# Attention layer of a hybrid decode step: turned weights fetched earlier, decode attention later, another order of output tiles

## The chip, the cores and the metric

The kernel runs on one core of one Trainium2 chip. The metric is the device time of one execution, in microseconds (us). The kernel before has a median of 1266.56 us over 3 runs (1266.55 to 1269.77).

## The reference, cut to what matters

A prompt of 1024 tokens and 8 single new tokens ("decode") go through two layers: a retention layer and a sliding-window attention layer (SWA). The change touches the SWA layer alone:

```
h = rmsnorm(x, g_norm); proj = h @ w_in                       # 1024 -> 1024 q, 128 k, 128 v, 1024 gate
q, k = rmsnorm per head (16 q heads of 64, 2 kv heads)
scores = q k^T / 8 - slope*dist, band of 128 keys back, one sink column per head
p = softmax(scores | sink);  o = p v                          # prompt, and likewise decode over cache_k, cache_v
y = x + (o * silu(gate)) @ w_out
```

All products must hold fp32 accuracy, so a projection is three matmuls: high part of the weights by high part of x, high by low, low by high (`proj`, L1698 to L1700).

## The kernel before, in words

The order of the work on each engine is written out by hand (a manual schedule): every engine's queue holds its instructions in the order in which the Python code emits them, and an engine waits at the head of its queue.

**Weights.** `wslot` (L1632) brings a block of 256 weight columns in four pieces of 256 KB. `load(i)` is a DMA on SP (SyncE's queue) into one of three buffers `wr` (L1642); `conv(i)` is a copy on ACT that makes the high part `wh` (L1648) and a subtraction on POOL that makes the low part `wl` (L1649). The fourth load needs a buffer that the first conversion has freed. A slot's steps stand in its list `todo`; `job()` takes from it up to the next `None` or to the next conversion, so a `None` is a pause of one job place.

**Projection tiles.** `group_proj` and later `so_all` are generators that emit projection tiles: a tile is 8 times the three matmuls into one of two PSUM banks `pj`. `fill(src, W)` pulls about W = 1.03 us of matmuls from them. A finished q tile is emptied by ACT (a square, L1915, and a scaled copy, L1916), a gate tile by DVE (L1930), then ACT (L1935) and DVE (L1941). `soon` and `now()` hold small pieces of work back to the next place.

**Attention.** 32 units of work ("duos": 4 head pairs pp by 8 chunks c of 128 tokens) go through one period each. In period m:

- PE: `att_o` of duo m-2 if its pp is odd (40 matmuls, L2108, which read the turned weights `R`), then `att_s` of duo m (scores, L2053), then four or five fills.
- DVE and ACT: `att_out` and `att_split` of duo m-2 (L2118, L2133, L2137 or L2141), `att_e` of duo m (bias and maximum, L2069 and L2074), `att_p` (four exponentials on ACT, L2080), `att_r` (reciprocal L2084, product on POOL L2085).
- `att_x` of the duo of period m-1: for even pp a DVE transpose into `pb` and a DMA of it to `pbs` in HBM (L2090, L2091); for odd pp a DMA of the even half back from `pbs` into `R` (L2094) and a DVE transpose of the odd half into `R` (L2095). `R` has two buffers.
- `ms_mm` and `ms_ev` (sums of squares of a q tile, L1991 to L2017) when a q pair is done; for the last third of the tokens (ti = 2) four small DMAs take the decode part `ms` to `ms16` (L2010).
- three job places a period, behind the first, second and fourth fill.

Decode attention is cut into steps (`dec_norm`, `dec_scores`, `dec_soft` 0 to 6, `dec_vload`, `dec_pt`, `dec_o`, `dec_out`; L2152 to L2229); the table `STEPS` says in which period and place each is emitted. `dec_out` sets `oready[2]`, without which no output tile of ti = 2 begins.

**Output tiles.** `so_all` emits 24 tiles (ft, ti): 8 blocks of 128 output columns by three groups of tokens. Each needs its residual loaded (`xr`, L2317), is summed on DVE (L2330), turned (L2260) and sent out in four DMAs (L2263). A tile with ti = 2 is also turned on PE (L104) for its decode rows.

When the last duo of group 0 is through, eight DMAs of 128 KB load the values of the second kv head (`kv_v4`, L1824).

Of the kernel before, what the change touches and what calls it, by code (L numbers as in the profile page):

```python
# [16 lines left out]
ND = 8  # L17
# [50 lines left out]
def _trunk(ctx, tc, nc, a):  # L68
# [1561 lines left out]
    def wslot(src, turn=True):  # L1630

        slot, box = [], {}  # L1632

        def first():
            box["hi"] = wp.tile([128, 8, 256], F32R, tag="wh", bufs=3, name="wh")
            box["lo"] = wp.tile([128, 8, 256], F32R, tag="wl", bufs=3, name="wl")
            slot[0:0] = (box["hi"], box["lo"])

        def load(i):
            raw = box[i] = wp.tile([128, 2, 256], F32, tag="wr", bufs=3, name="wr")  # L1640
            rows = src[256 * i:256 * i + 256]
            nc.sync.dma_start(out=raw, in_=rows.rearrange("(p u) f -> p u f", u=2) if turn else  # L1642
                              rows.rearrange("(k p) f -> p k f", p=128))

        def conv(i):
            js = slice(2 * i, 2 * i + 2)
            raw = box[i]
            nc.scalar.activation(box["hi"][:, js, :], raw, AF.Copy)  # L1648
            nc.gpsimd.tensor_tensor(box["lo"][:, js, :], raw, box["hi"].bitcast(F32)[:, js, :], ALU.subtract)  # L1649

        box["todo"] = [(first,), (load, 0), (load, 1), (load, 2), None, None, None, (conv, 0), (load, 3)] + [
            (conv, i) for i in range(1, 4)]
        jobs.append(box)
        slot.append(box)
        return slot
# [252 lines left out]
    def group_proj(gr):  # L1908

        def q_ev(pp, pl, ti, ps):  # L1910
            t0, t1 = TG[ti]
            n, npr = t1 - t0, min(t1, NP) - t0
            qs = Q[pp, ti, pl] = atp.tile([128, 384], F32, name="qs", bufs=6)
            sq = SQ[pp, ti, pl] = io("sq", 4)
            nc.scalar.activation(sq[:, :n], ps[:, :n], AF.Square)  # L1915
            nc.scalar.activation(qs[:, :npr], ps[:, :npr], AF.Copy, scale=gq)  # L1916
            if ti == 2:
                gs = slice(64 * gr, 64 * gr + 64)
                h = 4 * pp + 2 * pl
                nc.scalar.activation(Qd[gs, h, :], ps[lo_, 256:264], AF.Copy, scale=gq[lo_])  # L1920
                nc.scalar.activation(Qd[gs, h + 1, :], ps[hi_, 256:264], AF.Copy, scale=gq[hi_])
            if pl == 1:
                msq.append((pp, ti))

        def g_ev(pp, pl, ti, ps):
            t0, t1 = TG[ti]
            n, npr, nch = t1 - t0, min(t1, NP) - t0, chunks(ti)
            p = 2 * pp + pl
            gx = io("sq", 4)
            nc.vector.tensor_tensor(gx[:, :n], ps[:, :n], rbc[:, t0:t1], ALU.mult)  # L1930
            if p % 4 == 0:
                G[gr, ti] = atq[0].tile([128, 1536], F32, name="gt", bufs=2)
            gt = G[gr, ti].rearrange("p (n l x) -> p n l x", l=4, x=32)[:, 0:4 * nch, p % 4, :]
            gv = gx[:, :npr].rearrange("p (n x) -> p n x", x=32)
            nc.scalar.activation(gt, gv, AF.Tanh, scale=0.5)  # L1935
            gd, gxd = gdec2[:, p, :], gx[:, npr:n]
            if ti == 2:
                nc.scalar.activation(gd, gxd, AF.Tanh, scale=0.5)

            def rest():  # L1940
                nc.vector.scalar_tensor_tensor(gt, gt, 1.0, gv, ALU.add, ALU.mult)  # L1941
                if ti == 2:
                    nc.vector.scalar_tensor_tensor(gd, gd, 1.0, gxd, ALU.add, ALU.mult)
                    nc.vector.tensor_scalar(gd, gd, 0.5, None, ALU.mult)
            soon.append((rest,))

        a_, b_ = 2 * gr, 2 * gr + 1
        order = [("q", a_, 0), ("q", a_, 1), ("q", a_, 2), ("g", a_, 0), ("q", b_, 0), ("g", b_, 0), ("q", b_, 1),
                 ("q", b_, 2), ("g", a_, 1), ("g", b_, 1), ("g", a_, 2), ("g", b_, 2)]
        if gr == 0:  # L1950
            order.insert(10, ("q", 2, 0))
        else:
            order.pop(0)
        for kind, pp, ti in order:
            isq = kind == "q"
            t0, t1 = TG[ti]
            n = t1 - t0
            while 3 * (pp if isq else gr) + ti - (done["s"] if isq else done["o"]) >= (3 if isq else 2):
                yield 1e9
            for f in range(2):  # L1960
                ps = pjp.tile([128, 512], F32, tag="pj", name="pj")
                for k in range(8):
                    proj(ps[:, :n], slots[kind, pp], f, t0, t1, first=(k == 0), last=(k == 7), ks=[k])
                    if k < 7:
                        yield 3 * n / 2400.0
                (q_ev if isq else g_ev)(pp, f, ti, ps)
                if f == 1 and (kind, pp, ti) in nxt:
                    nxt[kind, pp, ti]()
                yield 3 * n / 2400.0
            if (kind, pp) == ("g", 3):  # L1970
                pend_r.append(ti)
# [29 lines left out]
    def ms_ev(xy, pp, ti, sq):  # L2001
        nch = chunks(ti)
        m = 32 * nch
        for j in range(2):
            nc.vector.transpose(sq[:, 192 * j:192 * j + 2 * m], xy[:, j, 320:320 + 2 * m])
        if ti == 2:
            ms = atp.tile([1, 2, 2, ND], F32, name="ms", bufs=1)
            nc.vector.tensor_copy(ms, xy[0:1, :, 448:464].rearrange("p j (l r) -> p l j r", l=2))
            for h in range(4):
                nc.sync.dma_start(out=ms16[4 * pp + h:4 * pp + h + 1, :], in_=ms[:, h // 2, h % 2, :])  # L2010
        rqf = atq[0].tile([128, 12], F32, name="rq", bufs=3)[:, 0:4 * nch]
        rq = rqf.rearrange("p (j l c) -> p j l c", j=2, l=2)
        mt = sq[:, 0:384].rearrange("p (j n) -> p j n", j=2)[:, :, 0:2 * m].rearrange(
            "p j (n i) -> p j n i", i=32)
        c0 = TG[ti][0] // 128
        for j in range(2):
            nc.vector.scalar_tensor_tensor(  # L2017
                rq[:, j], mt[:, j, :, 0].rearrange("p (l c) -> p l c", l=2), 1.0 / HD,
                e9[:, c0:c0 + nch].unsqueeze(1).broadcast_to([128, 2, nch]), ALU.mult, ALU.add)
        rsq(rqf, rqf, 4 * nch)  # L2020
        RQ[pp, ti] = rq
# [65 lines left out]
    def att_x(u):  # L2087
        if u.pp % 2 == 0:
            pb = atp.tile([128, 4, 160], F32, name="pb", bufs=1)
            nc.vector.transpose(pb, u.st[:, :, 0:160])  # L2090
            nc.sync.dma_start(out=pbs[u.c], in_=pb.rearrange("p h n -> p (h n)"))  # L2091
        else:
            u.pb = atp.tile([128, 2, 4, 160], F32, tag="R", name="R", bufs=2)
            nc.sync.dma_start(out=u.pb[:, 0].rearrange("p h n -> p (h n)"), in_=pbs[u.c])  # L2094
            nc.vector.transpose(u.pb[:, 1], u.st[:, :, 0:160])  # L2095

    def att_o(u):
        po = u.po = pvp.tile([128, 4, 512], F32, tag="o", name="o")
# [184 lines left out]
            nc.scalar.dma_start(out=y_s[:, 0, ft * 128:ft * 128 + 128], in_=yo[:8, 256:384])  # L2283

    def so_all():
        order = [(ft, ti) for ti in range(3) for ft in range(6)] + [(ft, ti) for ft in (6, 7) for ti in range(3)]
        early = []

        def start(ft, ti):
# [138 lines left out]
    dec_new()  # L2428
    while not msq:
        next(ps)  # L2430
    tq.close()
    xq_ = ExitStack()
    xyp = xq_.enter_context(tc.tile_pool(name="xyp", bufs=1, space=PSUM))
# [11 lines left out]
    def both():  # L2445
# [5 lines left out]
    W = 1.03  # L2451
    NU = len(duos)
    pend_m, x = [], None
    STEPS = {(30, 0): (dec_norm, 0), (30, 2): (dec_norm, 1), (30, 3): (dec_scores,), (30, 4): (dec_soft, 0),
             (31, 0): (dec_soft, 1), (31, 1): (dec_soft, 2), (31, 2): (dec_soft, 3), (31, 3): (dec_soft, 4),
             (31, 4): (dec_soft, 5), (32, 0): (dec_soft, 6), (32, 1): (dec_vload,), (33, 0): (dec_pt,), (33, 3): (dec_o,),
             (33, 4): (dec_out,)}

    def decode(m, s):
        if (m, s) in STEPS:  # L2460
            fn, *args = STEPS[m, s]
            fn(*args)

    for m in range(NU + 2):
        W = 0.95 if 16 <= m < 27 else 1.03
        u = duos[m] if m < NU else None
        w = duos[m - 2] if m >= 2 and duos[m - 2].pp % 2 else None
        if u:
            while (u.pp, u.ti) not in RQ:
                if msq:  # L2470
                    xy = xy_tile()
                    ms_ev(xy, *msq[0], ms_mm(xy, *msq.pop(0)))
                else:
                    next(ps)
        if w:
            assert (w.g, w.ti) in G
            att_o(w)
        if u:
            xy = xy_tile()
            att_s(u, xy)  # L2480
            if msq:
                pend_m.append((ms_ev, (xy, *msq[0], ms_mm(xy, *msq.pop(0)))))
        if w:
            att_out(w)
            att_split(w, 0)
# [29 lines left out]
        decode(m, 2)  # L2515
        fill(src, W)
        now()
        if u:
            att_r(u)
        decode(m, 3)  # L2520
# [53 lines left out]
```

## Time and profile before

| | us |
|---|---|
| median of 3 runs | 1266.56 |
| profiled execution | 1267.68 |
| span of its trace | 1265.9 |
| PE busy | 1224.4 (97%) |
| DVE, ACT, POOL busy | 743.2, 588.4, 688.7 |
| the stretch 880 to 1266 us (SWA layer): PE busy | 355.15 of 386.00 |
| the same: DVE, ACT, POOL busy | 194.86, 138.67, 140.36 |

The profile is of one execution. PE is busy almost throughout; the layer that the change touches takes the last 386 us. What is read below are the places in it where PE stands still or runs at half its clock. "a <- b" in a row of waits means that an instruction of a waited for b.

### The profile page before, as it was taken

What the parts mean: (1) busy time and instruction counts of PE and PEld (TensorE: products, weight loads), DVE (VectorE), ACT (ScalarE), POOL (GpSimd) and SP (SyncE); (2) the same over time, 40 slices, a digit from 0 to 9 for tenths busy, and PEclk for the clock granted to TensorE, in tenths of its full rate; (3) what the DMA queues carried; (4) which work ended last, traced back from release to release, by engine and by line L of the source; (5) the groups of instructions that cost most, each with busy time, mean ns of one, the idle gap of its engine ahead of it and who ended that gap; (6) DMA issues with size and microseconds to landing.
All of it is one profiled execution on the core that took longest, in us unless ns stands there. A gap on an engine that the chain in (4) does not pass through costs nothing.

```text
span 1265.9 us, 29416 instructions
## 1 busy us (share of the span) xinstructions
PE 1224.4 (97%) x11304; PEld 1159.7 (92%) x11304; DVE 743.2 (59%) x1462; ACT 588.4 (46%) x1482; POOL 688.7 (54%) x740
## 2 busy tenths in 40 slices
PE   7999999999999999999999999999999989987998
PEld 6999999999999999978889999999898978976998
DVE  7944655665565765377774566684265665667321
ACT  6533445454455554478772225454544454533000
POOL 6654444535458899889772357735555255334010
PEclk9999999999999999999999999999998999998999
DMA  6313867687666784465887955764322435153444
GB/s 219 110 59 121 256 183 227 195 252 211 196 205 192 225 231 133 124 207 175 259 249 193 294 166 183 232 191 118 108 76 95 119 114 145 68 193 106 112 106 88
DMA packets 260106, 213.10 MB, mean 168 GB/s; under 512 B 72905, under 2 KB 230981, under 8 KB 259950
## 3 DMA queue, kind: packets, MB, share of 16 engines
q1 hardware_dynamic: 210800, 178.16, 47.9%
q10 hardware_dynamic: 49166, 33.06, 8.8%
q8 instruction: 89, 1.46, 0.5%
q14 instruction: 51, 0.42, 0.1%
HBM read 139.03 MB, written 73.17 MB: 168 GB/s over the span
## 4 chain that ended last, share of the span: by engine, by line
PE 83%; DVE 5%; DMA 3%; POOL 3%; issue 3%; ACT 2%; SPq 1%; ACTq 0%; POOLq 0%; DVEq 0%
PE S L1317 9%; PE b L334 7%; PE b L336 7%; PE b L335 7%; PE pj L1698 6%; PE pj L1700 6%; PE pj L1699 5%; PE b L327 4%; PE b L328 4%; PE b L329 4%; PE tr L104 2%; PE o L2108 2%; PE b L543 2%; PE xy L2053 1%; DMA wr<-in_w_in_swa_dram 1%
## 5 line engine op out<-in xcount | busy, mean ns | idle before, releaser
L334 PE MATMUL b<-xh,woh 128*128 128x258 f32 x784 | 223.2, 285 | 0.0
L336 PE MATMUL b<-xh,wol 128*128 128x258 f32 x784 | 221.8, 283 | 0.2 <-POOL wol L225 0.2
L335 PE MATMUL b<-xl,woh 128*128 128x258 f32 x784 | 221.6, 283 | 0.0
L1698 PE MATMUL pj<-SA,wh 128*128 128x384 f32 (+1 forms) x576 | 193.4, 336 | 2.3 <-ACT qs L1916 2.1
L1700 PE MATMUL pj<-SA,wl 128*128 128x384 f32 (+1 forms) x576 | 187.6, 326 | 3.3 <-POOL wl L1649 3.3
L1699 PE MATMUL pj<-SA,wh 128*128 128x384 f32 (+1 forms) x576 | 187.0, 325 | 1.3 <-issue 1.3
L334 PEld LDWEIGHTS b<-xh,woh 128*128 128x128 f32 x784 | 148.0, 189 | 4.1 <-issue 4.1
L335 PEld LDWEIGHTS b<-xl,woh 128*128 128x128 f32 x784 | 148.7, 190 | 0.0
L336 PEld LDWEIGHTS b<-xh,wol 128*128 128x128 f32 x784 | 148.0, 189 | 0.4 <-POOL wol L225 0.4
L225 POOL TENSOR_TENSOR wol<-raw,woh 128x512 fp32r<-128x512 f32 x51 | 67.1, 1325 | 117.9 <-ACT woh L220 106.7
L327 PE MATMUL b<-woh,xh 128*128 128x256 f32 x448 | 126.6, 283 | 0.0
L328 PE MATMUL b<-wol,xh 128*128 128x256 f32 x448 | 126.0, 281 | 0.0
L329 PE MATMUL b<-woh,xl 128*128 128x256 f32 x448 | 125.6, 280 | 0.0
L1698 PEld LDWEIGHTS pj<-SA,wh 128*128 128x128 f32 x576 | 111.1, 193 | 11.1 <-issue 6.3
L1700 PEld LDWEIGHTS pj<-SA,wl 128*128 128x128 f32 x576 | 111.2, 193 | 5.1 <-POOL wl L1649 3.7
L1699 PEld LDWEIGHTS pj<-SA,wh 128*128 128x128 f32 x576 | 111.4, 193 | 0.0
L1649 POOL TENSOR_TENSOR wl<-wr,wh 128x512 fp32r<-128x512 f32 x48 | 62.6, 1319 | 83.6 <-ACT wh L1648 81.4
L327 PEld LDWEIGHTS b<-woh,xh 128*128 128x128 f32 x448 | 84.3, 188 | 5.0 <-issue 2.9
L329 PEld LDWEIGHTS b<-woh,xl 128*128 128x128 f32 x448 | 84.3, 188 | 0.0
L328 PEld LDWEIGHTS b<-wol,xh 128*128 128x128 f32 x448 | 84.3, 188 | 0.0
L2085 POOL TENSOR_TENSOR s<-s,sm 128x640 f32<-128x640 f32 x32 | 40.2, 1255 | 78.6 <-DVE sm L2084 78.6
L220 ACT ACTIVATE woh<-s 128x512 fp32r<-128x512 f32 x88 | 54.1, 624 | 58.0 <-POOL s L210 23.4
(515 smaller groups left out, 3173.8 us busy)
## 6 DMA issues: line engine op xcount, KB each, us to landing
raw<-in_w_in_ret_dram ACTq DMA_DIRECT2D x44, 512.0 KB
st<-in_state_ret_dram SPq DMA_DIRECT2D x64, 256.0 KB
out_dram<-st SPq DMA_DIRECT2D x64, 256.0 KB
vb<-vscr SPq DMA_DIRECT2D x64, 128.0 KB
evp<-qks SPq DMA_DIRECT2D x32, 256.0 KB
evx<-vsc SPq DMA_DIRECT2D x32, 256.0 KB
wr<-in_w_in_swa_dram SPq DMA_DIRECT2D x32, 256.0 KB
pbs<-pb SPq DMA_DIRECT2D x16, 320.0 KB
```

The source lines that it names most:

```text
L225: eng.tensor_tensor(lo, src_of(s, name, sub), hi.bitcast(F32), SUB)
L327: mm(dst, xh, wh, start=a and i == 0, stop=False, skip_group_check=True)
L328: mm(dst, xh, wl, start=False, stop=False, skip_group_check=True)
L329: mm(dst, xl, wh, start=False, stop=z, skip_group_check=True)
L334: mm(dst, wh, xh, start=a, stop=False, **sg)
L335: mm(dst, wh, xl, start=False, stop=False, **sg)
L336: mm(dst, wl, xh, start=False, stop=z, **sg)
L1317: mm(box[0], s.op[f"A{i + 1}{j + 1}", 0][w][:, k, :], xs_[t][x[j]][:, k, :], start=(xs_ is XH and w == 0 and j + k == 0), stop=(xs_ is XL ...
L1649: nc.gpsimd.tensor_tensor(box["lo"][:, js, :], raw, box["hi"].bitcast(F32)[:, js, :], ALU.subtract)
L1698: mm(ps, hi[:, k, fs], xh[:, k, t0:t1], start=first and k == ks[0], stop=False)
L1699: mm(ps, hi[:, k, fs], xl[:, k, t0:t1], start=False, stop=False)
L1700: mm(ps, lo[:, k, fs], xh[:, k, t0:t1], start=False, stop=last and k == ks[-1])
```

## The change

It has seven parts, all in the SWA layer: (1) one pause fewer between a slot's loads and its first conversion, and a fourth job place a period, behind the third fill; (2) a q pair is put on the list for `ms_mm` one place later, through `soon`; (3) the four DMAs of `ms` become one; (4) the DMA that fills `R` from `pbs` moves from `att_x`, in the period after a duo's scores, to the new `att_l`, right behind the scores; (5) `STEPS` puts decode attention into periods 31 to 35 (before: 30 to 33), and the loop runs two periods longer; (6) another order of output tiles; (7) guards that go with them.

```diff
-        box["todo"] = [(first,), (load, 0), (load, 1), (load, 2), None, None, None, (conv, 0), (load, 3)] + [
+        box["todo"] = [(first,), (load, 0), (load, 1), (load, 2), None, None, (conv, 0), (load, 3)] + [
             (conv, i) for i in range(1, 4)]
...
             if pl == 1:
-                msq.append((pp, ti))
+                soon.append((msq.append, (pp, ti)))
...
-            ms = atp.tile([1, 2, 2, ND], F32, name="ms", bufs=1)
-            nc.vector.tensor_copy(ms, xy[0:1, :, 448:464].rearrange("p j (l r) -> p l j r", l=2))
-            for h in range(4):
-                nc.sync.dma_start(out=ms16[4 * pp + h:4 * pp + h + 1, :], in_=ms[:, h // 2, h % 2, :])
+            ms = atp.tile([1, 4 * ND], F32, name="ms", bufs=1)
+            nc.vector.tensor_copy(ms.rearrange("p (l j r) -> p l j r", l=2, j=2),
+                                  xy[0:1, :, 448:464].rearrange("p j (l r) -> p l j r", l=2))
+            nc.sync.dma_start(out=ms16[4 * pp:4 * pp + 4, :], in_=ms)
...
         else:
+            nc.vector.transpose(u.pb[:, 1], u.st[:, :, 0:160])
+
+    def att_l(u):
+        if u.pp % 2:
             u.pb = atp.tile([128, 2, 4, 160], F32, tag="R", name="R", bufs=2)
             nc.sync.dma_start(out=u.pb[:, 0].rearrange("p h n -> p (h n)"), in_=pbs[u.c])
-            nc.vector.transpose(u.pb[:, 1], u.st[:, :, 0:160])
...
-        order = [(ft, ti) for ti in range(3) for ft in range(6)] + [(ft, ti) for ft in (6, 7) for ti in range(3)]
+        order = [(ft, 0) for ft in range(6)] + [(ft, 1) for ft in range(4)] + [(0, 2), (1, 2), (4, 1), (5, 1)] + [
+            (ft, 2) for ft in range(2, 6)] + [(ft, ti) for ft in (6, 7) for ti in range(3)]
...
-    STEPS = {(30, 0): (dec_norm, 0), (30, 2): (dec_norm, 1), (30, 3): (dec_scores,), (30, 4): (dec_soft, 0),
...
+    STEPS = {(31, 0): (dec_norm, 0), (31, 4): (dec_norm, 1), (32, 1): (dec_scores,), (32, 2): (dec_soft, 0),
+             (32, 4): (dec_soft, 1), (33, 1): (dec_soft, 2), (33, 2): (dec_soft, 3), (33, 3): (dec_soft, 4),
...
-    for m in range(NU + 2):
+    for m in range(NU + 4):
...
+        if u:
+            att_l(u)
         if w:
             att_out(w)
             att_split(w, 0)
...
         fill(src, W)
         now()
+        job()
         if u:
             att_r(u)
```

From here on a line number of the changed kernel is up to nine higher than that of the same code before (L2094 becomes L2098, L2095 becomes L2093, L2191 becomes L2194).

SP's queue around the first duos with odd pp (the trace of before shows it from 964 us on). `wr` are pieces of weights, `ms` the small decode sums, `R` the turned weights, `oscr` the split results of a duo. Before:

```order
L2091 DMA pbs<-pb 128x640 x6
L1642 DMA wr<-in_w_in_swa_dram 128x2x256 x3
L2010 DMA ms_11366<-ms 1x8x1 x4
L2094 DMA R<-pbs 128x640
L1642 DMA wr<-in_w_in_swa_dram 128x2x256
L2094 DMA R<-pbs 128x640
L2138 DMA oscr_h<-oh 128x4x128
```

The same queue of the changed kernel:

```order
L2091 DMA pbs<-pb 128x640 x6
L2098 DMA R<-pbs 128x640
L2091 DMA pbs<-pb 128x640
L1642 DMA wr<-in_w_in_swa_dram 128x2x256 x4
L2098 DMA R<-pbs 128x640
L2010 DMA ms_11366<-ms 4x1x8
L2098 DMA R<-pbs 128x640
L2141 DMA oscr_h<-oh 128x4x128
```

The first `R` now stands ahead of the pieces of weights and of `ms` (one DMA in place of four); all four pieces follow one another, since the first conversion comes sooner.

ACT's queue at the slot of the second gate block of group 1, behind the eight loads of values (the trace of before shows its conversions at 1056.92 us). Before:

```order
L1648 ACTIVATE wh<-wr 128x512
L2080 ACTIVATE s,sm<-s,mx 128x161 x2
L1935 ACTIVATE gt<-sq 128x12x32
L2080 ACTIVATE s,sm<-s,mx 128x161 x2
L1648 ACTIVATE wh<-wr 128x512 x2
L1935 ACTIVATE gt<-sq 128x12x32
L1648 ACTIVATE wh<-wr 128x512
```

The same place of the changed kernel:

```order
L1935 ACTIVATE gt<-sq 128x12x32
L1648 ACTIVATE wh<-wr 128x512 x2
L2080 ACTIVATE s,sm<-s,mx 128x161 x2
L1648 ACTIVATE wh<-wr 128x512
L2080 ACTIVATE s,sm<-s,mx 128x161 x2
L1648 ACTIVATE wh<-wr 128x512
L1935 ACTIVATE gt<-sq 128x12x32
```

The two conversions that come first stood behind the period's exponentials (L2080, four a period); now they stand ahead of them.

DVE's queue at the softmax of decode attention (`rbc`, `m`, `t`), the odd half of the turned weights (`R<-s`) and the output tiles (`sq<-pj`, `yo<-sq`). Before:

```order
L2179 TENSOR_TENSOR rbc<-rbc,ddec 16x1032
L2330 TENSOR_TENSOR sq<-pj,xr_15457 128x384
L2260 STREAM_TRANSPOSE yo<-sq 128x384
L2181 TENSOR_REDUCE m_11368<-rbc 16x8
L2182 TENSOR_SCALAR m_11368<-m_11368,skc 16x8
L2095 STREAM_TRANSPOSE R<-s 128x640
L2141 TENSOR_TENSOR SA<-ot,SA 128x4x128
L2184 TENSOR_TENSOR rbc<-rbc,m_11368 16x1032
L2084 RECIPROCAL sm<-sm 128x4
L2189 TENSOR_REDUCE t_11369<-rbc 16x8
```

In the changed kernel the last turn of a duo comes ahead of the whole softmax:

```order
L2093 STREAM_TRANSPOSE R<-s 128x640
L2144 TENSOR_TENSOR SA<-ot,SA 128x4x128
L2178 TENSOR_TENSOR rbc<-o,r_11367 16x8
L2179 TENSOR_TENSOR rbc<-o,r_11367 16x8x128
L2334 TENSOR_TENSOR sq<-pj,xr_15634 128x384
L2263 STREAM_TRANSPOSE yo<-sq 128x384
L2182 TENSOR_TENSOR rbc<-rbc,ddec 16x1032
L2121 SCALAR_TENSOR_TENSOR ot<-o,gt 128x512
L2184 TENSOR_REDUCE m_11368<-rbc 16x8
L2185 TENSOR_SCALAR m_11368<-m_11368,skc 16x8
L2144 TENSOR_TENSOR SA<-ot,SA 128x4x128
```

More of the change, by code (lines that the diff above doesn't have):

```diff
@@ L2430, in _trunk @@
         next(ps)
+        now()
     tq.close()
@@ L2453, in _trunk @@
     pend_m, x = [], None
-    STEPS = {(30, 0): (dec_norm, 0), (30, 2): (dec_norm, 1), (30, 3): (dec_scores,), (30, 4): (dec_soft, 0),
-             (31, 0): (dec_soft, 1), (31, 1): (dec_soft, 2), (31, 2): (dec_soft, 3), (31, 3): (dec_soft, 4),
-             (31, 4): (dec_soft, 5), (32, 0): (dec_soft, 6), (32, 1): (dec_vload,), (33, 0): (dec_pt,), (33, 3): (dec_o,),
-             (33, 4): (dec_out,)}
+    STEPS = {(31, 0): (dec_norm, 0), (31, 4): (dec_norm, 1), (32, 1): (dec_scores,), (32, 2): (dec_soft, 0),
+             (32, 4): (dec_soft, 1), (33, 1): (dec_soft, 2), (33, 2): (dec_soft, 3), (33, 3): (dec_soft, 4),
+             (33, 4): (dec_soft, 5), (34, 0): (dec_soft, 6), (34, 1): (dec_vload,), (34, 3): (dec_pt,), (35, 2): (dec_o,),
+             (35, 3): (dec_out,)}
     def decode(m, s):
@@ L2462, in decode @@
             fn(*args)
-    for m in range(NU + 2):
+    for m in range(NU + 4):
         W = 0.95 if 16 <= m < 27 else 1.03
         u = duos[m] if m < NU else None
-        w = duos[m - 2] if m >= 2 and duos[m - 2].pp % 2 else None
+        w = duos[m - 2] if 2 <= m < NU + 2 and duos[m - 2].pp % 2 else None
         if u:
@@ L2474, in _trunk @@
                     next(ps)
+                    now()
         if w:
```

## The prediction, put on record before the changed kernel was run

> **What bounds the kernel now.** I read the page first (busy times, clock), then the waits of PE in the SWA layer, then the granted clock around each wait, then the queues of SP, ACT and DVE at the places that these name.
>
> The page, its first lines: span, and the row of PE.
>
> ```profile
> span 1265.9 us, 29416 instructions
> PE 1224.4 (97%) x11304; PEld 1159.7 (92%) x11304; DVE 743.2 (59%) x1462; ACT 588.4 (46%) x1482; POOL 688.7 (54%) x740
> ```
>
> PE is the bound, and the change takes no matmul away. It can only win PE's idle time, and half-clock time that follows idle time. The waits of PE from 880 to 1266 us (waiting line, what ended the wait, us in total, times, longest):
>
> ```profile
> PE o L2108 <- DMA R<-pbs: 8.9, 4, 4.6
> PE o L2108 <- DVE t L2191: 6.9, 1, 6.9
> PE pj L1700 <- POOL wl L1649: 3.3, 1, 3.3
> PE pj L1698 <- ACT qs L1916: 2.1, 2, 1.8
> PE tr L104 <- ACT wh L1648: 2.0, 1, 2.0
> PE xy L1991 <- ACT sq L1915: 1.6, 1, 1.6
> PE pj L1699 <- issue: 1.3, 1, 1.3
> ```
>
> Together 26.1 us. Behind six of these waits the clock drops. The stretches that ran at half clock (window, length, then busy us and instructions of PE, PEld, DVE, ACT, POOL, then the granted clock):
>
> ```profile
> 974.50:981.33 6.83, 6.65 (x83) 5.76 (x84) 4.06 (x10) 2.26 (x7) 2.93 (x3) 0.50 0.39 121
> 1042.77:1046.18 3.41, 3.13 (x10) 3.14 (x11) 0.00 (x0) 0.00 (x0) 2.70 (x3) 0.50 0.45 140
> 1070.08:1073.49 3.41, 3.41 (x13) 3.41 (x12) 2.48 (x7) 1.76 (x8) 1.58 (x1) 0.50 0.01 5
> 1114.45:1117.86 3.41, 3.41 (x83) 2.50 (x69) 1.55 (x5) 0.63 (x1) 0.47 (x1) 0.50 1.03 380
> 1162.24:1172.48 10.24, 6.35 (x92) 6.05 (x93) 6.83 (x10) 2.50 (x4) 2.52 (x2) 0.50 0.76 211
> 1233.92:1237.33 3.41, 3.41 (x18) 3.41 (x17) 0.02 (x1) 0.27 (x1) 0.43 (x1) 0.50 0.72 148
> ```
>
> PE is busy for 26.4 us in them; at full clock that is half, so 13.2 us are lost. Idle and half clock make 39.3 us: that is all that the change can win, about 3%. The waits of 1.6 and 2.0 us were each followed by a stretch of 3.41 us, which costs 1.7 us; behind those of 1.3 and 1.8 us no such row stands. So length alone doesn't decide near 1.6 us; I count 1.7 us with every wait of 2 us or more, and half of it below.
>
> The Trainium skill ("TensorE: Matmul & The Clock Gate", section "HAM oscillation") gives the rule "no PE-idle gaps >~3.4µs". By it only two of the six drops, those after 4.6 and 6.9 us, should be there; the trace shows drops behind 1.6 to 3.3 us too, and the measurement decides. By that rule 8.3 us less would go and 0.8 us less come back in the sum below, so that it would end at 1247 us.
>
> **The change part by part.**
>
> *Turned weights one period earlier.* Before, the DMA stood behind the weights' pieces and behind four small DMAs (SP's queue, start and time of the issue, and the matmul that waited):
>
> ```profile
> 968.63 2.77 SPq L2010 DMA_DIRECT2D ms<-ms  x4
> 971.50 0.39 SPq L2094 DMA_DIRECT2D R<-pbs  x1
> 974.68 1.20 PE L2108 MATMUL o<-R,V 32*64 32x128 f32 x28 [2.79 <-DMA R<-pbs]
> 982.42 0.45 SPq L2094 DMA_DIRECT2D R<-pbs  x1
> 991.04 0.46 SPq L2094 DMA_DIRECT2D R<-pbs  x1
> ```
>
> From issue to use it needed 3.2 us. A period is 8.6 us (982.42 to 991.04). Now it is issued a period and a fill earlier, right behind the scores, so it leads by some 9 us more; the latest arrival before was 4.6 us late. All four waits end: 8.9 us idle, and 6.65/2 + 3.41/2 = 5.0 us of half clock, 13.9 us. The two buffers of `R` don't undo it: the one that is needed is freed by `att_o` at the head of the same period, which PE does before the scores. What queues on SP behind that wait is `ms`, pieces of weights and `oscr`, for the length of one `att_o` (28 of its 40 matmuls took 1.20 us above, so 1.7 us), and nobody on PE waits for those within a period. The one DMA for `ms` in place of four saves SP some 2.1 us (2.77 to a quarter), off PE's path but for the place above.
>
> *Decode attention later.* Before, PE's longest wait was for a transpose that stood behind softmax pieces on DVE:
>
> ```profile
> 1158.31 1.17 DVE L2181 TENSOR_REDUCE m<-rbc 16x8 f32<-16x1032 f32 x1
> 1159.65 0.82 DVE L2095 STREAM_TRANSPOSE R<-s 128x640 f32<-128x640 f32 x1
> 1160.99 1.21 DVE L2184 TENSOR_TENSOR rbc<-rbc,m 16x1032 f32<-16x1032 f32 x1
> 1165.88 0.19 DVE L2191 RECIPROCAL t<-t 16x8 f32<-16x8 f32 x1
> ```
>
> The order now has the last turn of a duo ahead of every softmax piece, so the 6.9 us and 6.35/2 = 3.2 us go: 10.1 us. What is late next are the small PE transposes of the probabilities, which stand two places behind the last softmax piece (1.2 us for each wide DVE operation above), and the load of the cached values. The trace has no such wait; its bounds are 0 and about 3 us (a load of 256 KB takes 3.3 us, below). I take 1.5 us, nearer to the softmax row.
>
> *Earlier conversions, four job places.* At the first gate slot of group 1 the conversions now come well before their use: the wait for `wl`, 3.3 + 3.13/2 = 4.9 us, goes. The wait of the tail (L104 behind `wh`), 2.0 + 1.7 = 3.7 us, goes with the order of output tiles: the last slot is asked for two output tiles earlier before its use, and its pieces have landed when ACT gets there. The wait of L1991 for a square on ACT, 1.6 + 1.7 = 3.3 us, goes with `soon`: the sums are emitted a fill later than the square.
>
> But an earlier conversion also reaches its piece before it has landed, and ACT then stands with all that is queued behind it. A piece alone (SP's issue, and the ACT copy that waited for it):
>
> ```profile
> 1043.02 0.55 SPq L1642 DMA_DIRECT2D wr<-in_w_in_swa_dram  x1
> 1046.32 0.63 ACT L1648 ACTIVATE wh<-wr 128x512 fp32r<-128x512 f32 x1 [4.05 <-DMA wr<-in_w_in_swa_dram]
> ```
>
> 3.3 us; the conversion now stands two job places behind the loads: two fills of 1.03 us, so 2.1 us, or more where a period's scores lie between. So ACT waits 1 us or so at a slot, before the four exponentials of a period, and the reciprocal on DVE waits with them. Two banks of `pj` cover it: a tile is 24 matmuls, 0.18 us apart:
>
> ```profile
> 1046.31 0.34 PE L1698 MATMUL pj<-SA,wh 128*128 128x384 f32 x1
> 1046.49 0.33 PE L1699 MATMUL pj<-SA,wh 128*128 128x384 f32 x1
> ```
>
> so PE has 4.3 us before it needs a bank back. One slot is worse, the second gate slot of group 1, whose pieces queue behind the eight loads of values:
>
> ```profile
> 1045.47 6.41 SPq L1824 DMA_DIRECT2D V<-vscr  x8
> 1050.40 0.43 ACT L2080 ACTIVATE s<-s,mx 128x161 f32<-128x161 f32 x1 [3.45 <-DVE mx L2074]
> 1051.97 2.00 SPq L1642 DMA_DIRECT2D wr<-in_w_in_swa_dram  x3
> 1056.92 1.28 ACT L1648 ACTIVATE wh<-wr 128x512 fp32r<-128x512 f32 x2 [3.41 <-DMA wr<-in_w_in_swa_dram]
> ```
>
> The piece comes 11.5 us after the first of the eight, and ACT had already waited 3.4 us for it. Now the conversion stands ahead of the exponentials that began at 1050.40. ACT, free from 1046.95 on (3.45 us earlier), then stands for 6.5 us at least and 10.0 us at most; I take 8, between them, which is 3.7 us more than the banks cover. With 1.7 us of half clock that is 5.4 us; the bounds are 0 (the old wait of 3.4 us was followed by no wait of PE as long) and 10.0 - 4.3 + 1.7 = 7.4 us.
>
> The Trainium skill ("DMA: Bandwidth & Descriptors", section "Queues, rings and completion order") says that on each DMA engine descriptors are consumed in ring order, and that SP owns one ring on each. That speaks against this part: moving the conversion up cannot bring the piece up. The trace agrees: 5.0 us from issue to use behind the eight loads, 3.3 us alone.
>
> *First period.* The 1.8 us for `qs` stays and grows: a third conversion now stands ahead of that copy on ACT and POOL. Rows of one each, as a group with its mean in ns:
>
> ```profile
> L1648 ACT ACTIVATE wh<-wr 128x512 fp32r<-128x512 f32 x43 | 25.9, 622 | 22.3 <-DMA wr<-in_w_in_swa_dram 14.3 <-DMA wr<-in_w_out_swa_dram 6.8 <-ACT yo L2269 0.7
> L1649 POOL TENSOR_TENSOR wl<-wr,wh 128x512 fp32r<-128x512 f32 x43 | 56.2, 1323 | 82.6 <-ACT wh L1648 80.4 <-DMA out_dram<-yo 1.9
> ```
>
> between 0.6 and 2.0 us; I take 1.3, and half of a 1.7 us half-clock stretch, which is as likely as not: 2.1 us.
>
> *Nothing.* The rest is reordering on engines that are half idle. The 1.3 us of "issue" stays.
>
> **The sum.** Away: 13.9 + 10.1 + 4.9 + 3.7 + 3.3 = 35.9 us. Back: 1.5 + 5.4 + 2.1 = 9.0 us. The profiled execution took 1267.68 us, so 1267.7 - 35.9 + 9.0 = 1240.8 us; the median stands 1.1 us below the profiled execution, hence 1239.7 us.
>
> **The rivals.**
>
> *All goes and nothing comes back.* For it: ACT is busy for a third of the layer (window, length, then busy us of PE, PEld, DVE, ACT, POOL).
>
> ```profile
> 880.00:1266.00 386.00, 355.15 (x4493) 332.83 (x4492) 194.86 (x481) 138.67 (x453) 140.36 (x124) 0.96 0.41 112
> ```
>
> Against: the wait of 3.41 us above gets longer by construction. 1266.6 - 35.9 = 1230.7 us.
>
> *Some slots stall.* Ten slots are converted earlier, nine beside the one priced. If ACT's waits outlast the banks at five of them, each at the price of L1991's wait (1.6 + 1.7 = 3.3 us), 16.5 us come back: 1256.2 us. For it: 3.3 us to land against 2.1 us between load and conversion. Against: in the trace ACT waits of 3.4 and 4.05 us are not followed by as long a wait of PE.
>
> *Slower: the conversions stall PE at nearly every slot.* The same mechanism at the price of the `wl` wait, 4.9 us (3.3 + 1.6): nine times that is 44.1 us, 1283.8 us. It is slower than before by over 0.3% from seven of the nine on (1239.7 + 7 × 4.9 = 1274.0 us; six give 1269.1). For it: a blocked ACT holds the exponentials, the q tiles' copies and the gates' tanh at once. Against: the covers of 4.3 us, and ACT catches up.
>
> *The turned weights come no earlier.* If SP stands at the head of the period waiting for a buffer or a piece of weights, the 13.9 us stay: 1253.6 us. The order speaks against it: the pieces now stand behind `R`.
>
> **The chances.** Forecast 0.55, all goes 0.12, some slots 0.20, slower 0.06, weights no earlier 0.07. About 0.3%, 3.8 us, is what a measurement of this kernel can tell from no change. Slower by more: 0.06. Within: 0.07 (a quarter of the case of some slots, if nearly six stall or cost more, and a little of the last). Faster: 0.87. The range reaches from the best case, 1230 us, to the case of five slots, 1256 us: it leaves out the slower case, a part of the some-slots case and the edge of the best, under 2 in 10.
>
> **What would show it.** Right: no PE wait of L2111 for `R<-pbs`; the first DMA of `R` some 9 us earlier in its period; no wait of `att_o` on softmax pieces; PE waits behind ACT around the eight loads of values, 4 us there, and under 2 us at the other slots; five or so half-clock stretches gone. Wrong: PE waits for `qs`, `gt` or `sq` at several slots, each with an ACT copy L1648 that waits for `wr` just before it; or a wait for `R<-pbs` that stays; or waits of output tiles for residuals or for `dec_out`.

## The result and the profile after

The changed kernel takes 1259.24 us (median of 6 runs, 1259.04 to 1262.77), the kernel before in the same comparison 1267.01 us: a ratio of 0.994, 95% interval 0.9917 to 0.9963. It is faster, but by 7.8 us where 27 were forecast, and it lies above the range. The profiled execution took 1262.77 us, 3.5 us over the median; its span is 1261.0 us. One execution in a run below, of 6674.55 us, was slow and is left out of that run's median.

The busy times on its page:

```profile
PE 1220.8 (97%) x11304; PEld 1155.4 (92%) x11304; DVE 752.9 (60%) x1462; ACT 587.6 (47%) x1482; POOL 689.5 (55%) x740
```

The waits of PE in the same layer (from 880 us to the end):

```profile
PE pj L1698 <- ACT qs L1916: 9.8, 3, 4.8
PE pj L1698 <- DVE sq L1930: 3.6, 1, 3.6
PE o L2111 <- issue: 3.3, 4, 1.0
PE o L2111 <- DVE R L2093: 1.9, 1, 1.9
PE tr L104 <- ACT yo L2272: 1.7, 1, 1.7
PE xy L104 <- DVE rbc L2196: 1.4, 1, 1.4
PE xy L1991 <- ACT sq L1915: 0.5, 1, 0.5
```

The rows of `att_o` for `R<-pbs` and for `t`, and the one for `wl`, are gone. The row for q tiles grew from 2.1 to 9.8 us, the tail (L104) kept 1.7 of its 2.0 us, and new rows stand beside them: 22.2 us in sum against 26.1. The stretches at half clock:

```profile
914.40:921.23 6.83, 5.99 (x81) 5.29 (x82) 1.85 (x7) 2.66 (x10) 1.25 (x1) 0.50 0.00 1
1044.11:1047.52 3.41, 3.30 (x70) 3.06 (x78) 0.18 (x1) 2.04 (x9) 1.25 (x1) 0.50 0.27 77
1071.42:1074.83 3.41, 3.28 (x38) 2.79 (x39) 2.25 (x3) 3.23 (x12) 2.80 (x2) 0.50 0.01 2
1184.06:1187.47 3.41, 3.41 (x13) 3.41 (x12) 0.00 (x0) 0.00 (x0) 0.00 (x0) 0.50 0.78 213
```

PE is busy for 16.0 us in them, so 8.0 us are lost, against 13.2 before. Idle and half clock fell from 39.3 to 30.2 us, 9.1 us, where the medians differ by 7.8 us and the two profiled executions by 4.9 us. Ahead of 880 us, where nothing was changed, PE stood idle for 13.0 us in this execution against 10.8 before, which takes 2.2 us of the gain back; the other 2 us are not placed. So the gain is small mainly because new waits came, not because the old ones stayed.

What ACT waited for, two rows from the same stretch of the kernel before and then of the changed one (pieces of the input weights, pieces of the output weights):

```profile
ACT wh L1648 <- DMA wr<-in_w_in_swa_dram: 14.3, 6, 4.0
ACT wh L1648 <- DMA wr<-in_w_out_swa_dram: 6.8, 4, 3.0
```

```profile
ACT wh L1648 <- DMA wr<-in_w_in_swa_dram: 29.3, 11, 6.2
ACT wh L1648 <- DMA wr<-in_w_out_swa_dram: 7.9, 4, 3.1
```

ACT stands twice as long for pieces of the input weights. The longest wait of PE, around 1040 us, shows how the earlier conversions reach it. Queue by queue: SP issues the fourth piece, ACT makes three copies in a row, POOL's queue, ACT's copy that waited for the fourth piece, DVE's maximum that waited for POOL's memsets, ACT emptying a q tile, and PE's matmul that waited for its bank:

```profile
1036.35 0.55 SPq L1642 DMA_DIRECT2D wr<-in_w_in_swa_dram  x1
1034.32 1.66 ACT L1648 ACTIVATE wh<-wr 128x512 fp32r<-128x512 f32 x3
1035.03 2.55 POOL L1649 TENSOR_TENSOR wl<-wr,wh 128x512 fp32r<-128x512 f32 x2 [4.65 <-ACT wh L1648]
1037.53 1.25 POOL L2085 TENSOR_TENSOR s<-s,sm 128x640 f32<-128x640 f32 x1
1038.74 1.27 POOL L1649 TENSOR_TENSOR wl<-wr,wh 128x512 fp32r<-128x512 f32 x1
1039.95 1.55 POOL L2073 MEMSET s<- 32x512 f32 x4
1039.81 0.63 ACT L1648 ACTIVATE wh<-wr 128x512 fp32r<-128x512 f32 x1 [3.30 <-DMA wr<-in_w_in_swa_dram]
1041.53 0.82 DVE L2074 TENSOR_REDUCE mx<-s 128x4 f32<-128x644 f32 x1 [5.45 <-POOL s L2073]
1043.60 0.56 ACT L1916 ACTIVATE qs<-pj,gq 128x384 f32<-128x384 f32 x1
1044.22 0.59 PE L1698 MATMUL pj<-SA,wh 128*128 128x264 f32 x1 [4.80 <-ACT qs L1916]
```

This is a head pair's first chunk, whose scores are masked by four memsets on POOL. They stand behind three subtractions and a product, which take POOL from 1035.03 to 1039.99 us; the maximum waits for them, the exponentials for the maximum, and the q tile's copy stands behind the exponentials in ACT's queue. PE needs the bank and waits 4.8 us. Here the three copies ahead did not wait for their pieces: what holds the memsets is that three subtractions now come closely together. With the old spacing (the first run below) none stands right ahead of them, and the maximum waits 1.64 us there, not 5.45. The fourth piece held ACT too, for 3.30 us, but that wait was over (1040.44) before the maximum was there. In the first period (4.49 us) the same chain begins with a wait of ACT for its pieces, of 2.59 us.

### The profile page after: what moved, and what is told of

Same layout as the page of the kernel before. It is cut to its first block, busy times and chain, and to the rows that moved or that the text cites. A ratio compares the mean times of both kernels' runs of the same rounds, so it can differ in the third digit from the quotient of the medians.

```text
span 1261.0 us, 29403 instructions
## 1 busy us (share of the span) xinstructions
PE 1220.8 (97%) x11304; PEld 1155.4 (92%) x11304; DVE 752.9 (60%) x1462; ACT 587.6 (47%) x1482; POOL 689.5 (55%) x740
## 5 line engine op out<-in xcount | busy, mean ns | idle before, releaser
L1698 PE MATMUL pj<-SA,wh 128*128 128x384 f32 (+1 forms) x576 | 192.3, 334 | 13.7 <-ACT qs L1916 9.8
L1698 PEld LDWEIGHTS pj<-SA,wh 128*128 128x128 f32 x576 | 110.0, 191 | 23.2 <-ACT qs L1916 10.5
L225 DVE TENSOR_TENSOR wol<-s,woh 128x512 fp32r<-128x512 f32 x88 | 67.4, 769 | 20.0 <-ACT woh L220 19.7
```

The lines of the kernel that those rows point to most:

```text
L225: eng.tensor_tensor(lo, src_of(s, name, sub), hi.bitcast(F32), SUB)
L1698: mm(ps, hi[:, k, fs], xh[:, k, t0:t1], start=first and k == ks[0], stop=False)
```

## The experiments

The theory: pieces of weights are now reached before they have landed, ACT stands at them, and POOL's and ACT's other work stands behind. The rival: the earlier conversions are a gain, and what was lost lies in the other parts. All times are medians; the interval is that of the ratio to the kernel before, which had medians of 1267.0 to 1268.0 us in these comparisons. A difference of 2 or 3 us between two versions is near what this can tell.

**Conversions as before, all else changed.**

```diff
-        ... (load, 2), None, None, (conv, 0), ...
+        ... (load, 2), None, None, None, (conv, 0), ...
...
-        job()      # behind the third fill
```

> The changed kernel with three pauses and three job places a period again, all else as changed. Theory (pieces of weights are reached before they have landed; ACT stands, POOL's subtractions stand behind it, and POOL's other work behind those): the first period's wait falls from 4.5 us to about 1.8 and loses its half-clock stretch, the one at the eight loads from 3.6 to about 2, the 4.8 us for a q tile turns back into the 3.3 us for wl, so about 10 us less than the changed kernel, 1249 us. Rival (the earlier conversions are a gain, the losses come from the other parts): same or slower, 1259 to 1264 us.

Measured: 1246.69 us, ratio 0.9839 (0.9815 to 0.9863). The earlier conversions cost 12.5 us. ACT's wait for pieces of the input weights and PE's waits that are left:

```profile
ACT wh L1648 <- DMA wr<-in_w_in_swa_dram: 9.7, 5, 2.5
```

```profile
PE pj L1698 <- ACT qs L1916: 3.7, 2, 2.0
PE o L2111 <- issue: 2.4, 1, 2.4
PE pj L1700 <- POOL wl L1649: 1.8, 1, 1.8
PE xy L104 <- DVE rbc L2196: 1.1, 1, 1.1
PE xy L1991 <- ACT sq L1915: 1.1, 1, 1.1
```

So the loss goes with the earlier conversions; which link of the theory carries it, the next runs separate. The wait for `wl` is back, with 1.8 us and not 3.3. The 1.9 us for the transpose L2093 are gone, but the 2.4 us that are put down to "issue" are of the same kind: the matmul starts at 1142.55 us, 0.11 us after another of these transposes has ended (1141.60 + 0.84 us).

**The earlier conversions alone, in the kernel before.**

```diff
-        ... (load, 2), None, None, None, (conv, 0), ...
+        ... (load, 2), None, None, (conv, 0), ...
...
+        job()      # behind the third fill
```

> The kernel before with the one pause less and the fourth job place alone. Theory (earlier conversions reach pieces that have not landed, whatever else is changed): slower than before by 4 to 10 us, 1271 to 1277 us, with waits of PE for q tiles of 4 to 5 us at the first period and at the first chunk after the third slot, and the wait for wl gone. Rival (they only hurt together with the other parts): 1262 us, since the wait for wl, 4.9 us, goes.

Measured: 1277.91 us, ratio 1.0086 (1.0059 to 1.0112), 9.9 us slower than before. PE's longest waits:

```profile
PE o L2108 <- DMA R<-pbs: 14.4, 4, 5.2
PE pj L1698 <- DVE sq L1930: 5.5, 1, 5.5
PE o L2108 <- DVE R L2095: 4.4, 1, 4.4
PE tr L104 <- DVE yo L2260: 3.3, 1, 3.3
PE pj L1698 <- ACT qs L1916: 3.2, 1, 3.2
```

So this part is a loss with or without the others. The wait for `wl` is gone, as forecast. The waits at the places named are there in part: 3.2 us in the first period, but 4.4 us around 1040 us stand at `att_o`, for the odd half's transpose, and not at a q tile.

**The two halves of that part.** Three pauses with four job places, then two pauses with three places:

```diff
+        ... (load, 2), None, None, None, (conv, 0), ...     # first run
...
-        job()                                               # second run, behind the third fill
```

> The changed kernel with three pauses again, but four job places. If the distance from loads to the first conversion is what costs (theory): a pause more puts the conversion a job place later, so most of the 12.5 us that undoing both gave come back, 1248 to 1251 us. Rival (the fourth job place packs loads, conversions and subtractions more closely whatever the distance): 1256 to 1260 us.

> The changed kernel with three job places a period again, but two pauses. Theory (distance): two pauses at three places a period are nearly the distance of three pauses at four, so much the same as the run with three pauses and four places, 1248 to 1252 us. Rival (it is the pauses alone): 1257 to 1260 us.

Measured: 1256.59 us (ratio 0.9903, 0.9883 to 0.9924) and 1251.80 us (0.9872, 0.9853 to 0.9892). Against 1259.2 the pause gives back 2.7 us and the place 7.4 us; both together 12.5. (The first of these is near the noise: its interval and that of the changed kernel overlap.) The second run lies where the theory put it, but the first should have equalled it and is 4.8 us slower, inside the rival's range. In the first run PE's longest wait, 4.08 us, stands at `att_o`, and it too begins with a piece that had not landed. ACT's copy is of a fourth piece; DVE's gate product waits for the tanh (L1935) behind that copy; the odd half's transpose on DVE stands behind the product and ends at 987.25 us:

```profile
980.93 0.63 ACT L1648 ACTIVATE wh<-wr 128x512 fp32r<-128x512 f32 x1 [4.16 <-DMA wr<-in_w_in_swa_dram]
982.01 1.34 DVE L1941 SCALAR_TENSOR_TENSOR gt<-gt,sq 128x384 f32<-128x384 f32 x1 [4.58 <-ACT gt L1935]
987.36 1.54 PE L2111 MATMUL o<-R,V 32*64 32x128 f32 x80 [4.08 <-issue]
```

A pause ahead of the first conversion moves the first three pieces away from their loads, but not the fourth, which is loaded behind that conversion. The fourth job place brings its load and its conversion closer together, and it also packs a slot's subtractions more closely on POOL, as around 1040 us above. So the theory, told as the distance from the loads to the first conversion, was too narrow. How the 7.4 us divide between the fourth piece and the packing, these two runs don't show.

**The last piece later.** Only the fourth piece's conversion is moved, two job places on (with a line of `job()` that lets it pass a pause there); the next slot's steps move on with it:

```diff
-            (conv, i) for i in range(1, 4)]
+                       (conv, 1), (conv, 2), None, None, None, (conv, 3)]
```

> The changed kernel with the conversion of each slot's fourth piece two job places later, the first three as changed. Theory (ACT and with it POOL stand for the fourth piece, whose load starts only when the first conversion has freed a buffer): the waits of 4.5 and 4.8 us for q tiles shrink to 1 to 3 us and lose half clock, 5 to 7 us less than the changed kernel, 1253 us, though wl may be waited for. Rival (the first three pieces are what ACT stands for): within 2 us of 1259 us.

Measured: 1252.14 us, ratio 0.9879 (0.9857 to 0.9901): 7.1 us of the 12.5 hang on the conversion of the one piece whose load starts only when the first conversion has freed a buffer. The two waits for q tiles became 3.0 us (first period) and 2.0 us; the one at the eight loads, where the first pieces are late, stayed, 3.5 us.

**The masking on DVE.**

```diff
-                nc.gpsimd.memset(st[32 * b:32 * b + 32, :, 0:128 - 32 * b], NEG)
+                nc.vector.memset(st[32 * b:32 * b + 32, :, 0:128 - 32 * b], NEG)
```

> The changed kernel with the masking of a head pair's first chunk (four memsets, L2073) on DVE in place of POOL. Theory (the memsets stand on POOL behind a subtraction that waits for a piece of weights, and maximum, exponentials and the emptying of q tiles wait for them): the waits of 4.5 and 4.8 us for q tiles lose about 4 us each and their half-clock stretches, about 9 us less than the changed kernel, 1250 us. Rival (the exponentials stand behind the conversion on ACT anyway): within 2 us of the changed kernel.

Measured: 1256.12 us, ratio 0.9912 (0.9888 to 0.9936), 3.1 us better than the changed kernel; the two waits fell from 4.49 to 3.26 and from 4.80 to 2.74 us. The intervals of the two kernels overlap, so the 3.1 us are near the noise; the two waits are clearer. They lie between the two forecasts: the memsets are one link of the chain, but the exponentials stand behind the copy that waits for the fourth piece in any case. In this run's trace that copy begins at 1036.41 us, after 3.31 us of waiting, the exponentials follow at 1036.95, and PE gets its bank at 1038.76. So of the 4.8 us about 2 came from the subtractions ahead of the memsets, and the rest from the fourth piece.

**The values later.**

```diff
         if later_v4:
-            later_v4.clear()
-            kv_v4(0, 1)
-            kv_v4(1, 1)
...
+            later_v4.append(1)
+            if len(later_v4) == 3:
+                later_v4.clear()
+                kv_v4(0, 1)
+                kv_v4(1, 1)
```

> The changed kernel with the eight loads of the second head's values issued a period and a half later, behind the pieces of weights that they stood ahead of. Theory (the pieces queue behind the eight loads): the wait of 3.6 us at that slot and its half clock go, 5 to 6 us less than the changed kernel, 1254 us. Rival (ACT reaches the pieces too early in any case, 3.3 us from issue to landing): 0 to 2 us less, 1258 us.

Measured: 1255.67 us, ratio 0.9902 (0.9882 to 0.9922), 3.6 us better, between the two forecasts; here too the intervals overlap a little. The price that I had put on the place is seen in the changed kernel: the eight loads, the pieces behind them, ACT's wait, PE's wait.

```profile
1054.28 6.26 SPq L1824 DMA_DIRECT2D V<-vscr  x8
1060.63 2.03 SPq L1642 DMA_DIRECT2D wr<-in_w_in_swa_dram  x3
1065.80 1.26 ACT L1648 ACTIVATE wh<-wr 128x512 fp32r<-128x512 f32 x2 [6.20 <-DMA wr<-in_w_in_swa_dram]
1069.94 0.44 PE L1698 MATMUL pj<-SA,wh 128*128 128x384 f32 x1 [3.62 <-DVE sq L1930]
```

In the run with the values later the 3.6 us for `sq` are gone, and 1.2 us for L1991 stand there.

**Values later, masking on DVE and conversions as before, together.** The two edits above and the first one.

> The changed kernel with conversions as before, the masking of the first chunks on DVE and the values a period and a half later. In the run with conversions as before 12.7 us of PE's idle time are left, 3.7 of them for q tiles and 1.1 at the slot behind the values; if the two edits still find what they are for, 3 to 5 us less than 1246.7: 1242 to 1244 us. Rival (with the old distance neither matters): 1246 to 1247 us.

Measured: 1246.92 us, ratio 0.9835 (0.9818 to 0.9852), the same as conversions as before alone. With the old spacing the two edits find nothing to win.

**The order of output tiles as before.**

```diff
-        order = [(ft, 0) for ft in range(6)] + [(ft, 1) for ft in range(4)] + [(0, 2), (1, 2), (4, 1), (5, 1)] + [
-            (ft, 2) for ft in range(2, 6)] + [(ft, ti) for ft in (6, 7) for ti in range(3)]
+        order = [(ft, ti) for ti in range(3) for ft in range(6)] + [(ft, ti) for ft in (6, 7) for ti in range(3)]
```

> The changed kernel with the order of output tiles of before. If the new order bought what I priced (3.7 us at the tail): 2 to 4 us slower than the changed kernel, since 1.7 us of that wait stand there still. Rival (it bought nothing, the wait of the tail only changed its cause): within 1 us of 1259 us.

Measured: 1260.62 us, ratio 0.9946 (0.9929 to 0.9963). The interval covers the changed kernel's ratio; whether the new order is worth 1.4 us or nothing stays open. The 3.7 us that I priced are not seen: the tail's wait is 1.8 us with the old order and 1.7 us with the new one.

**Decode attention as before,** with conversions as before: `STEPS` is that of before.

> Conversions as before, and decode attention in periods 30 to 33 again. If moving it bought what I priced (10.1 us away, 1.5 back): 1254 to 1256 us, with one wait of att_o of 6 to 7 us behind softmax pieces. Rival (the wait only moved, to the scores of decode attention, its small transposes and the load of values, 3 us in sum in the run at 1246.7 us): 1248 to 1251 us.

Measured: 1248.28 us, ratio 0.9842 (0.9824 to 0.9860), against 1246.69 us without this edit: 1.6 us, within the intervals. No wait of 6 to 7 us came back; PE's longest rows in this run:

```profile
PE o L2111 <- issue: 4.4, 2, 3.2
PE pj L1698 <- DVE sq L2334: 3.7, 3, 1.7
```

The 4.4 us of "issue" are decode attention's all the same. The wait of 3.2 us ends at 1138.74 us, 0.11 us after the DVE product that reads the decode scores out of the one buffer of `o`; the other, of 1.3 us, ends 0.10 us after a transpose that stood behind three softmax pieces. But the run without this edit has 4.7 us of waits at its own decode steps (2.4, 0.7, 1.1 and 0.4 us), so the move bought nothing that these runs can tell. And the 6.9 us were not the softmax's.

**Turned weights as before,** with conversions as before: the DMA stands in `att_x` again.

> Conversions as before (the run at 1246.7 us), and the DMA of the turned weights back in the period after the scores. If fetching them earlier bought what I priced (13.9 us): 1258 to 1261 us, with waits of PE for R<-pbs of 8 us or more in sum. Rival (it bought little, since the transpose of the odd half is due at the same time): 1248 to 1252 us.

Measured: 1260.86 us (nine executions, 1257.04 to 1266.00), ratio 0.9951 (0.9930 to 0.9972): the earlier fetch is worth 14.2 us there. PE waits for `R<-pbs` again, 10.5 us in three waits, the longest of 4.8 us.

**The earlier fetch alone, in the kernel before.**

```diff
+    def att_l(u):
+        if u.pp % 2:
             u.pb = atp.tile([128, 2, 4, 160], F32, tag="R", name="R", bufs=2)
             nc.sync.dma_start(out=u.pb[:, 0].rearrange("p h n -> p (h n)"), in_=pbs[u.c])
...
+        if u:
+            att_l(u)
```

> The kernel before with the earlier DMA of the turned weights alone; decode attention, conversions and output tiles as before. If the 6.9 us wait that the profile of before puts down to a softmax piece was a wait for the DMA of the turned weights (issued at 1161.42 us, behind pieces of weights): no wait of att_o of more than 2 us is left, and 8.9 + 6.9 us idle with half clock go, 1242 to 1248 us less than 20 us below before at most, so 1247 to 1250 us. Rival (it was the transpose behind the softmax on DVE): that wait stays at 6 to 7 us, 13.9 us less than before, 1253 to 1255 us.

Measured: 1246.96 us, ratio 0.985 (0.9807 to 0.9892), 20.0 us less than before (13.7 to 24.5 by the interval): as much as the best version with all parts. PE's waits:

```profile
PE pj L1700 <- POOL wl L1649: 3.6, 2, 3.3
PE pj L1698 <- ACT qs L1916: 2.4, 2, 1.5
PE tr L104 <- DVE sq L2333: 1.9, 2, 1.7
PE xy L1991 <- ACT sq L1915: 1.6, 1, 1.6
PE o L2111 <- issue: 1.6, 1, 1.6
```

The 6.9 us are gone with decode attention where it always was. The 1.6 us of "issue" are what is left at that place: the matmul starts at 1144.83 us, 0.10 us after the odd half's transpose, which still stands behind a softmax piece. No version run beats 1246.7 us; the fetch alone reaches it with one edit.

## Why the prediction was wrong, point by point

26.9 us were forecast and 7.8 measured. About half of what is missing is the earlier conversions, which cost 12.5 us where the sum had 2.6. The other half are the remaining parts: with the old spacing they brought 20.9 us (1267.59 to 1246.69) where the sum had 29.5 (35.9 less 4.9 for `wl`, and less the 1.5 that was to come back).

**Turned weights: right in kind.** No wait for `R<-pbs` is left. Priced at 13.9 us, measured 20.0 alone and 14.2 beside the others. But the fetch also took most of the wait of the next point, so the 20.0 us stand against both prices, 13.9 + 10.1 = 24.0 us. In the changed kernel part of it came back: the odd half's transpose, delayed on DVE, is what `att_o` waits for next (1.9 us and four waits of 3.3 us in sum; each ends within 0.1 us of such a transpose), which I had not priced. One of the four, with the transpose that ends at 1151.45 us:

```profile
1150.60 0.85 DVE L2093 STREAM_TRANSPOSE R<-s 128x640 f32<-128x640 f32 x1
1151.55 1.42 PE L2111 MATMUL o<-R,V 32*64 32x128 f32 x80 [0.95 <-issue]
```

**Decode attention: the failed reading of a label.** The step "PE's longest wait was for a transpose that stood behind softmax pieces" is wrong. The rows of before said so. That transpose had ended at 1160.47 us (it is in the prediction's rows), `att_o` doesn't read the softmax's reciprocal, and the DMA of `R` was issued after that:

```profile
1160.93 0.40 SPq L1642 DMA_DIRECT2D wr<-in_w_out_swa_dram  x1
1161.42 0.41 SPq L2094 DMA_DIRECT2D R<-pbs  x1
1166.13 1.16 PE L2108 MATMUL o<-R,V 32*64 32x128 f32 x32 [6.93 <-DVE t L2191]
```

From issue to use 4.7 us, where 3.2 were read at 971 us. The profile names as releaser what ended last, at 1166.07 us, by chance. PE stood from 1159.20 us on, so the transpose can explain the first 1.3 us of the wait, and the DMA the other 5.7. The runs with decode attention back (1.6 us) and with the fetch alone (1.6 us of the wait left, behind the transpose) show that most of the 10.1 us belonged to the fetch.

**Earlier conversions: the term that failed most.** The prediction had "away" 4.9 us for `wl` and "back" 5.4 + 2.1 us, a cost of 2.6 us in sum; measured 9.9 us alone and 12.5 beside the rest. The step "two banks of `pj` cover it" failed. It set ACT's wait against PE's banks and left out the chain between: subtractions on POOL, memsets and products behind them, maximum, exponentials, q tile. Of the places, the one at the eight loads came out as priced (3.6 us idle and 3.28/2 = 1.6 us of half clock, 5.3 us against 5.4), by the path that was named: ACT, the exponentials, the reciprocal, which waited 8.31 us. The size is partly luck: ACT stood for 6.2 us and not 8, and by the prediction's own subtraction of 4.3 us only 1.9 us of idle time would have come through. The first period was 4.5 us and not 1.8 + 1.3, with 6.83 us of half clock; the wait for `wl` turned into one of 4.8 us for a q tile at the same place. The rival "some slots stall", at 1256 us, came nearest, with three places in place of six, at more each; that its time came out so near is luck, since the other parts brought less than its sum has.

**The tail and the square.** Both were to go, for 3.7 + 3.3 us. The tail's wait (L104) stayed, 1.7 us with another releaser; with the old spacing it is 0.6 us. The square's wait went from 1.6 to 0.5 us, but is 1.1 us with the old spacing, so it shrank and did not go. All parts but the earlier conversions together (1246.7 us) bring no more than the fetch alone (1247.0 us). The later square was not tried alone, the order of tiles not to better than its interval.

**The clock.** The prediction counted 1.7 us of half clock with every wait of 2 us or more. On the whole that held: the waits of 4.5, 4.8 and 3.6 us were followed by drops, the first by one of 6.83 us. But in the same trace a wait of 1.4 us (for `rbc`) was followed by a drop, and waits of 1.9 us (`R`, L2093) and 1.7 us (the tail) by none. It isn't a threshold, see below.

## What to carry to other kernels

Before an operation that is moved up is priced, ask whether its input has landed by then: an engine that runs its queue in order and reaches a load early makes everything behind it wait, also on the engines that it feeds. Follow such a wait through each in-order queue to the bound engine; a cover of two buffers counts only if nothing else stands between. And check each releaser's name against the operands of the waiting instruction: where the named one isn't read by it, look for a DMA that was issued in time to end there.

## What the runs showed of the hardware that was not expected

A DVE operation can last as long as the operations that POOL runs at the time. In the run with decode attention as before, a subtraction on DVE, 0.65 us at its median, took 3.79 us while POOL ran three:

```profile
1131.82 3.79 DVE L2144 TENSOR_TENSOR SA<-ot,SA 128x512 fp32r<-128x512 f32 x1
1131.29 3.76 POOL L1649 TENSOR_TENSOR wl<-wr,wh 128x512 fp32r<-128x512 f32 x3
```

The Trainium skill ("SBUF — State Buffer", section "SBUF: two separate sides") says that DVE, with two inputs from SBUF, and POOL share a port pair that the first holds for its whole instruction. The trace agrees in kind, but here the DVE operation lasted through the rest of three POOL instructions and ended 0.56 us after the last.

The clock does not follow from a wait's length alone. In the run with the values later a wait of 3.45 us was followed by no drop; nor was one of 3.33 us in the run with the fetch alone, though before a wait of the same length at the same place was. The wait, then what followed it, in the run with the fetch alone:

```profile
1033.07:1036.41 3.34, 0.01 (x2) 0.00 (x1) 1.24 (x4) 2.52 (x9) 3.34 (x3) 1.00 0.00 0
1036.41:1043.00 6.59, 6.29 (x97) 5.29 (x98) 2.44 (x8) 0.89 (x2) 4.93 (x4) 1.00 0.84 222
```

So the same wait can cost 1.7 us more or nothing, and a difference of that size between two versions need not come from what the edit was meant to do.
